# First FFN of a decoder trunk with three pairs of blocks by eight products instead of two, and the low parts of the first gated input's weights made by VectorE and by adding DMAs instead of GpSimd

## The chip, the cores and the metric

The kernel runs on one core of a Trainium2 chip. The metric is the device time of one execution in microseconds (us). The core has a TensorE for matrix products (PE in the profile, its weight loads PEld), VectorE (DVE), ScalarE (ACT), GpSimd (POOL) and SyncE (SP, which here only issues loads). Each takes its own instructions in order and waits for the others at semaphores.

## The reference, cut to what matters

Two layers over 512 tokens of width 1024, everything in float32. Each layer has a half-step gated FFN, a token mixer (retention in the first layer, forgetting attention in the second), another half-step FFN, and a gated input from `p`:

```python
def swiglu(x, w_in, w_out):
    g, u = jnp.split(x @ w_in, 2, axis=-1)
    return (jax.nn.silu(g) * u) @ w_out

h = x
for i in range(DEPTH):                     # DEPTH = 2
    nw = norm_w[i]
    h = h + 0.5 * swiglu(rmsnorm(h, nw[0]), ffn_w_in[i, 0], ffn_w_out[i, 0])
    hn = rmsnorm(h, nw[1])
    h = h + (retention(hn, ...) if i % 2 == 0 else forgetting_attention(hn, ...))
    h = h + 0.5 * swiglu(rmsnorm(h, nw[2]), ffn_w_in[i, 1], ffn_w_out[i, 1])
    gate = jax.nn.sigmoid(rmsnorm(h, nw[3]) @ ple_w_gate[i])
    h = h + gate * (p[i] @ ple_w_proj[i])
return rmsnorm(h, final_norm_w)
```

So there are four FFNs (1024 to 2 x 2816 and back), called 0 to 3 here and "first" to "fourth", and two gated inputs. FFN 0 is the first work of the kernel. The first gated input stands between FFN 1 and FFN 2.

## The kernel before, in words

**Products in three.** The activations lie transposed in SBUF, `h` as eight blocks of 128 features by 512 tokens. Every float32 operand is split into a high part (rounded to the PE's faster float32r) and a low part (the operand less its high part), and a product is made of three matmuls: high by high, high by low, low by high. So each block of weights (128 by 1024, 512 KB, loaded by SP into one of four `wraw` buffers, L76) needs a cast for its high part, on ScalarE (L83), and a low part, in one of two ways. `split` subtracts (L84) on the engine in `W.low`, which is VectorE or, in the mixers and the gated inputs, GpSimd. `negated` writes the negated weights by a second ScalarE pass (L125 is the cast there, L126 the negation) and adds the weights to them by a DMA that reads them a second time and adds on arrival, issued by GpSimd (L127). High and low part go into one of three `w8` buffers (`w` in the profile's rows); the weights are asked for in the order of `W.plan`, a look-ahead of two chunks ahead of their use (`W.look`). A chunk in `W.placed` goes into other buffers than `w8`.

**The FFN's first product.** The 22 column blocks of gate and up are made in 22 "pairs" (gate and up of one block). A pair is a 2 by 2 block product (two halves of the features by two halves of the tokens), and it is made in one of two forms.
- `plain` (L543) makes it by eight block products, 96 matmuls of 256 columns. It needs the normed activations in their plain forms alone, and the weights as two chunks, each with high and low part.
- `start`, `one`, `two`, `three` and `finish` (matmuls in `product`, L508) make it by seven block products, 84 matmuls, in Winograd's way: it needs sums and differences of weight blocks (four sums on VectorE, L157, each split by ScalarE and VectorE into the buffers `s12` and `s34`; a fifth block in `a12` by an adding DMA), and sums and differences of activation blocks (the forms t1 to t4 by `Norm.quarters`, L387 to L420). The results are put together in PSUM by VectorE and ScalarE (L561 to L580).

The first pairs of each FFN are plain, `PLAIN[i]` of them, since the forms take VectorE a while to make; the others are of the seven-product form. The weights of two pairs after the plain ones (and of two at each later seam) are `direct`: their low part is made by subtraction. For each pair `gated` then makes silu(gate) times up (L585 to L590) and splits it; it needs the rows of the norm (`n.rows`), one per token. Those come from sums of squares over the features: `columns` sums them on PE (L337) and takes the root (L479 to L487), and `rows` turns the columns into rows on PE (L474, copied at L468). A plain pair holds two of PSUM's eight banks from its first matmul until it is gated, and a pair of the seven-product form likewise.

**The order at the start of FFN 0.** The input blocks and the first pair's weights arrive in pieces while pair 0 is made. Pair 1's two chunks go into `w8`: the first at once, the second into the buffer that pair 0 gives back. Between pair 0 and pair 1 PE makes the columns. After ten of the sixteen steps of pair 1 it turns them into rows and gates pair 0. Then come pair 2's `one` and `two`, the gating of pair 1, and then, pair by pair, `one` and `two` of the next before `three` of the last.

**The first gated input.** `ple` with `parts == 1` makes eight column blocks of `gate` (24 matmuls each, `ple_g`) and of the added part (6 each, `ple_p`). For each block m, `step` multiplies with the rows (L1131), takes the sigmoid (L1132), multiplies (L1140), adds to `h[m]` (L1141), and makes the forms of block m - 1 for the norm of FFN 2 (`nxt.block`, `corner`: L316, L317, L387 to L420, L440 to L447). Meanwhile `W.low` is GpSimd. From block 4 on the look-ahead is two longer, and the first pair of FFN 2 is placed in buffers that its sums don't use yet (`place_first`: `s34` three times and `a12` once). FFN 2 then runs like FFN 0, with its plain pairs ordered so that the last two feature blocks come last.

**Who orders what.** PE's order is the program's. The order of the other engines' instructions and of the loads is made at build time by a planner from the program's order and its own estimates.

Of the kernel before, what the change touches and what calls it, by code (L numbers as in the profile page):

```python
# [26 lines left out]
FH = 16  # L27
LOOKAHEAD = 2
KEPT = 7
PLAIN = (2, 2, 2, 2)  # L30
CHUNKS = [((0, 6), (6, 14), (14, 22)) for n in PLAIN]
H2 = S // 2
HALVES = (slice(0, H2), slice(H2, S))
# [2 lines left out]
class Pair:  # L36
# [3 lines left out]
    def __init__(self, ffn, q, r):  # L40
        self.ffn, self.q, self.r, self.direct = ffn, q, r, False
# [13 lines left out]
class Weights:  # L55
# [3 lines left out]
    def __init__(self, tc, raw_pool, pool):  # L59
        self.tc, self.nc, self.raw_pool, self.pool = tc, tc.nc, raw_pool, pool  # L60
        self.plan, self.ready, self.used = [], [], 0
        self.low = self.nc.vector
        self.limit, self.spare = None, []
        self.look, self.placed = LOOKAHEAD, {}
        self.sum_pool, self.open_ffn, self.pairs_used = None, None, 0
        self.ahead, self.behind = 0, ()

# [9 lines left out]
        return raw  # L77

    def split(self, raw, hi, lo, src=None):
        if self.low is None and src is not None:  # L80
            self.negated(raw, hi, lo, src)
            return
        self.nc.scalar.copy(hi, raw)  # L83
        self.low.tensor_tensor(out=lo, in0=raw, in1=hi.bitcast(F32), op=ALU.subtract)  # L84

    def chunk(self, src):
        n = src.shape[1]
        raw = self.load(src)
        if id(src) in self.placed:
            hi, lo = (t.rearrange("p a c -> p (a c)") for t in self.placed.pop(id(src))())  # L90
            self.split(raw, hi, lo)
            return hi, lo
        if self.spare:
            tiles = [self.spare.pop(0)() for _ in range(4)]
            for i in range(2):
                self.split(raw[:, 512 * i : 512 * (i + 1)], tiles[i], tiles[2 + i])
            return Halves(tiles[0:2]), Halves(tiles[2:4])
        t = self.pool.tile([P, 2, 1024], F32R, name="w8")
        self.split(raw[:, :n], t[:, 0, :n], t[:, 1, :n], src)
        return t[:, 0, :], t[:, 1, :]  # L100
# [71 lines left out]
    def open(self, ffn, pool):  # L172
        self.open_ffn, self.sum_pool, self.pairs_used, self.ahead, self.behind = ffn, pool, 0, 0, ()

    def place_first(self, pair):

        tile = lambda n, b: self.sum_pool.tile([P, 2, 512], F32R, name=n, bufs=b)
        self.placed[id(pair.q)] = lambda: (tile("s34", 3), tile("s34", 3))
        self.placed[id(pair.r)] = lambda: (tile("s34", 3), tile("a12", 2))
# [19 lines left out]
def trunk(ctx, tc, a):  # L199
    nc = tc.nc  # L200
# [15 lines left out]
    W = Weights(tc, wraw, wpool)  # L216

    def unit(pool):
        return pool.tile([P, S], F32R, name="unit_" + {id(ua): "a", id(ub): "b", id(uc): "c", id(ud): "d"}[id(pool)])


    ffn_src = []
    for i in range(4):
        ins = [Pair(i, a["ffn_w_in"][i, m, 0], a["ffn_w_in"][i, m, 1]) for m in range(NF)]
        chunks = CHUNKS[i]
        outs = [[a["ffn_w_out"][i, m][:, k0 * P : k1 * P] for m in range(KB)] for k0, k1 in chunks]
        for m in [PLAIN[i]] + [k1 + 1 for _, k1 in chunks[:-1]]:
            ins[m].direct = ins[m + 1].direct = True
# [11 lines left out]
    def plan_ffn(i):  # L240
        ins, outs = ffn_src[i]
        at = PLAIN[i]
        for pair in ins[:at]:
# [54 lines left out]
    def bank():  # L298
        return psum.tile([P, S], F32, name="bank")
# [44 lines left out]
    class Norm:  # L344
# [17 lines left out]
        def plain(self, b):  # L362

            g = self.gain[:, b : b + 1]
            if b % 2:
                hi, lo = self.unit(), self.unit()
                split(h[b], hi, lo, g)
                both = [(hi[:, c], lo[:, c]) for c in HALVES]
            else:
                both = []  # L370
                for i, c in enumerate(HALVES):
                    u = self.unit() if i == 0 else unit(ud)
                    both.append(tuple(u[:, d] for d in HALVES))
                    split(h[b][:, c], *both[i], g)
            n = 1 + b % 2
            if n == 1:
                self.forms.append({})
            self.forms[b // 2].update({f"b{n}1": both[0], f"b{n}2": both[1]})
# [139 lines left out]
    def ffn(i, n, nxt, stack, apool, meanwhile=None):  # L518


        ins, outs = ffn_src[i]
# [1 line left out]
        c0, c1 = HALVES  # L523
        live, act = {}, {}

        def plain(m, between=None):

            ws = [W.take(ins[m].q), W.take(ins[m].r)]
            g, u = bank(), bank()
            order = [(k, t) for k in range(KB) for t in range(2)]  # L530
            if i == 2:
                order.sort(key=lambda kt: (kt[0] >= KB - 2, kt[1]))
            elif i:
                order.sort(key=lambda kt: kt[1])
            for at, (k, t) in enumerate(order):
                if at == 10 and between:
                    between()
                e = k % 2
                for o, (w, c) in ((g, (ws[e], 0)), (u, (ws[1 - e], 512))):
                    ks = slice(c + k // 2 * P, c + (k // 2 + 1) * P)  # L540
                    xh, xl = n.forms[k // 2][f"b{1 + e}{1 + t}"]
                    for q, (x, y) in enumerate(((w[0], xh), (w[0], xl), (w[1], xh))):
                        nc.tensor.matmul(  # L543
                            o[:, HALVES[t]], x[:, ks], y, start=k == t == q == 0, stop=k == KB - 1 and q == 2,
                            skip_group_check=True,
                        )
            return g, u
# [61 lines left out]
                    nxt.block(m)  # L609

        done = PLAIN[i]
        whole = [plain(m) for m in range(done - 1)]
        n.columns()
        W.begin((n.last,) if n.early else ())

        def scaled():
            n.rows()
            for m, (g, u) in enumerate(whole):
                gated(m, g, u, True)

        last = plain(done - 1, scaled)
        start(done)
        one(done)
        two(done)
# [2 lines left out]
        for c, (k0, k1) in enumerate(chunks):  # L627
# [8 lines left out]
            done = k1  # L636
# [451 lines left out]
    def ple(l, n, nxt, phi, plo, parts=1):  # L1088

        w = S // parts  # L1090
        with ExitStack() as pools:
# [12 lines left out]
            for part in range(parts):  # L1104
# [52 lines left out]

                m = 0
                if part == 0:
                    W.low = nc.gpsimd  # L1160
                    os = [added(m) for m in range(2 + parts)]
                    gs = gates((0,)) if parts == 1 else gates((0, 1, 2, 3))
                    n.columns()
                    m = len(gs)
                    gs += gates((m,))
                    n.rows()
                    if parts == 1:
                        os += [added(3)]
                        rest(0, gs[0], os[0])
                        gs += gates((2,))  # L1170
                        rest(1, gs[1], os[1])
                        gs += gates((3,))
                    for m in range(2 if parts == 1 else 0, 4):
                        rest(m, gs[m], os[m])
                    m = 4
                    if parts > 1:
                        rest(4, gs[4], added(4))
                        m = 5
                if parts == 1:
                    W.look = LOOKAHEAD + 2  # L1180
                    W.place_first(ffn_src[2][0][0])
                while m < KB:
                    g = gates((m,))[0]
                    rest(m, g, added(m))
# [189 lines left out]
```

## Time and profile before

| | us |
|---|---|
| median of three runs | 2192.59 (2189.26 to 2194.67) |
| the profiled execution | 2193.35 |
| its span in the profile | 2191.5 |
| PE busy | 2142.5 (98%) |
| VectorE busy | 1454.5 (66%) |
| ScalarE busy | 1202.4 (55%) |
| GpSimd busy | 472.6 (22%) |

The profile is of one execution; its times count from the start of the span. In its rows a group or an instruction is named by line, engine, operation, and output<-inputs; "[... <-X]" gives the idle time of the engine just before it and what ended that. A row of a table by stage reads: stretch, length, then busy time and count of instructions for PE, PEld, VectorE, ScalarE and GpSimd, then the granted clock of PE as a share of full speed, the DMA engines' share and GB/s. A row of waits reads: who waited, for whom, us in total, times, the longest.

### The profile page before, as it was taken

How to read it: one execution, taken by the hardware profiler on the slowest of the kernel's cores; microseconds unless marked ns; L12 is line 12 of the kernel's file. 1: busy time of each engine (PE TensorE's matmuls, PEld its weight loads, DVE VectorE, ACT ScalarE, POOL GpSimd, SP SyncE). 2: the span in 40 equal slices, each digit the busy share in tenths (PEclk: the TensorE clock that was granted, in tenths of full speed). 3: DMA queues.
4: the chain of work that ended last, by engine and by line, in shares of the span. 5: the costliest groups of instructions: out<-in, count | busy, mean ns of one | idle time of the engine just before them, and what ended most of it. 6: DMA issues, size and time to landing. Idle time of an engine off the chain costs nothing.

```text
span 2191.5 us, 34456 instructions
## 1 busy us (share of the span) xinstructions
PE 2142.5 (98%) x13525; PEld 1927.9 (88%) x13525; DVE 1454.5 (66%) x2629; ACT 1202.4 (55%) x2027; POOL 472.6 (22%) x354
## 2 busy tenths in 40 slices
PE   8999999999999999999998999999999999999997
PEld 7999997888888798989988999898788899999987
DVE  8686766352533677767758687775675696777765
ACT  7465553433333574745556556464787774655544
POOL 0010003444344000101142011012334200100055
PEclk9999999999999999999999999999999999999999
DMA  5465562222222244746523555463622144654631
GB/s 174 124 167 148 140 164 97 82 95 77 94 77 87 77 128 132 177 119 152 144 94 97 129 160 149 137 167 105 152 81 88 67 125 114 161 154 139 155 106 40
DMA packets 85315, 267.08 MB, mean 122 GB/s; under 512 B 9360, under 2 KB 12944, under 8 KB 85152
## 3 DMA queue, kind: packets, MB, share of 16 engines
q1 hardware_dynamic: 63328, 209.78, 28.2%
q0 software_dynamic: 20592, 54.01, 14.6%
q8 instruction: 106, 1.74, 0.3%
q10 hardware_dynamic: 1232, 1.09, 0.1%
q14 instruction: 57, 0.47, 0.1%
HBM read 262.71 MB, written 2.13 MB: 121 GB/s over the span
## 4 chain that ended last, share of the span: by engine, by line
PE 85%; DVE 6%; ACT 4%; DMA 2%; issue 2%; POOL 1%; SPq 0%; ACTq 0%; DVEq 0%; POOLq 0%
PE bank L508 33%; PE bank L325 14%; PE bank L323 14%; PE bank L324 13%; PE bank L543 4%; PE bank L703 2%; PE bank L702 2%; PE bank L704 2%; DMA wraw<-in_ffn_w_in 1%; ACT p L1006 1%; DVE w L84 1%; ACT p L1008 1%; ACT w L83 1%; DVE tlo L314 1%; PE bank L337 0%
## 5 line engine op out<-in xcount | busy, mean ns | idle before, releaser
L83 ACT CAST w<-wraw 128x1024 fp32r<-128x1024 f32 (+1 forms) x240 | 243.4, 1021 | 420.0 <-PE bank L325 254.9
L325 PE MATMUL bank<-unit_a,w 128*128 128x512 f32 x736 | 287.2, 390 | 4.3 <-DVE w L84 2.6
L323 PE MATMUL bank<-unit_a,w 128*128 128x512 f32 x736 | 288.5, 392 | 1.9 <-ACT w L83 1.6
L324 PE MATMUL bank<-unit_a,w 128*128 128x512 f32 x736 | 286.7, 390 | 0.2 <-DVE unit_a L314 0.2
L84 POOL TENSOR_TENSOR w<-wraw,w 128x1024 fp32r<-128x1024 f32 x93 | 226.8, 2442 | 259.3 <-ACT w L83 246.8
L83 ACT CAST s<-sums 128x512 fp32r<-128x512 f32 x320 | 191.8, 617 | 153.4 <-DVE sums L157 107.4
L325 PE MATMUL bank<-unit_d,w 128*128 128x512 f32 (+1 forms) x712 | 268.2, 377 | 4.6 <-DVE w L84 4.6
L323 PE MATMUL bank<-unit_d,w 128*128 128x512 f32 (+1 forms) x712 | 269.3, 378 | 3.2 <-ACT w L83 1.6
L324 PE MATMUL bank<-unit_d,w 128*128 128x512 f32 (+1 forms) x712 | 268.0, 376 | 1.8 <-DVE unit_d L314 1.8
L84 DVE TENSOR_TENSOR s<-sums,s 128x512 fp32r<-128x512 f32 x320 | 214.1, 685 | 75.8 <-ACT s L83 75.3
L127 POOL DMA_DIRECT2D a<-in_ffn_w_in x80 | 70.3, 878 | 643.4 <-ACT a L126 422.0
L84 DVE TENSOR_TENSOR w<-wraw,w 128x1024 fp32r<-128x1024 f32 (+1 forms) x147 | 173.3, 1184 | 19.5 <-ACT w L83 19.3
L508 PE MATMUL bank<-unit_b,s 128*128 128x256 f32 x880 | 184.4, 276 | 0.7 <-DVE bank L565 0.7
L508 PE MATMUL bank<-unit_d,s 128*128 128x256 f32 x1140 | 178.4, 276 | 0.0
L508 PE MATMUL bank<-unit_a,s 128*128 128x256 f32 x1260 | 175.0, 276 | 1.4 <-ACT unit_a L387 0.9
L604 DVE SCALAR_TENSOR_TENSOR tmp<-bank,rows 128x512 f32<-128x512 f32 x96 | 66.0, 689 | 164.9 <-PE bank L325 163.7
L325 PEld LDWEIGHTS bank<-unit_a,w 128*128 128x128 f32 x736 | 138.1, 188 | 35.5 <-DVE w L84 4.3
L323 PEld LDWEIGHTS bank<-unit_a,w 128*128 128x128 f32 x736 | 138.2, 188 | 32.2 <-ACT w L83 3.5
L324 PEld LDWEIGHTS bank<-unit_a,w 128*128 128x128 f32 x736 | 138.2, 188 | 28.5 <-DVE unit_a L314 0.5
L325 PEld LDWEIGHTS bank<-unit_d,w 128*128 128x128 f32 x712 | 134.3, 189 | 30.7 <-DVE w L84 6.6
L323 PEld LDWEIGHTS bank<-unit_d,w 128*128 128x128 f32 x712 | 134.4, 189 | 30.2 <-ACT w L83 3.3
L508 PEld LDWEIGHTS bank<-unit_a,s 128*128 128x128 f32 x1260 | 158.0, 188 | 1.8 <-ACT unit_a L387 1.1
(292 smaller groups left out, 4787.9 us busy)
## 6 DMA issues: line engine op xcount, KB each, us to landing
wraw<-in_ffn_w_in SPq DMA_DIRECT2D x174, 512.0 KB, 4.3
wraw<-in_ffn_w_out SPq DMA_DIRECT2D x64, 512.0 KB, 4.7
w<-in_ffn_w_in POOLq DMA_DIRECT2D x56, 512.0 KB, 5.4
a<-in_ffn_w_in POOLq DMA_DIRECT2D x80, 256.0 KB, 6.3
wraw<-in_ffn_w_out SPq DMA_DIRECT2D x32, 384.0 KB, 3.7
wraw<-in_ret_qk SPq DMA_DIRECT2D x16, 512.0 KB, 3.5
wraw<-in_ret_v SPq DMA_DIRECT2D x16, 512.0 KB, 3.6
wraw<-in_ret_g SPq DMA_DIRECT2D x16, 512.0 KB, 3.5
```

The costliest lines, as they stand in the source:

```text
L83: self.nc.scalar.copy(hi, raw)
L84: self.low.tensor_tensor(out=lo, in0=raw, in1=hi.bitcast(F32), op=ALU.subtract)
L127: self.nc.gpsimd.dma_start(out=lo, in_=src, accum_op=ALU.add)
L323: nc.tensor.matmul(out, wh, xh, start=first, stop=False)
L324: nc.tensor.matmul(out, wh, xl, start=False, stop=False)
L325: nc.tensor.matmul(out, wl, xh, start=False, stop=last)
L508: add = lambda w, x, start, stop: nc.tensor.matmul(out, w, x, start=start, stop=stop, skip_group_check=True)
L543: nc.tensor.matmul(o[:, HALVES[t]], x[:, ks], y, start=k == t == q == 0, stop=k == KB - 1 and q == 2, skip_group_check=True,)
L604: nc.vector.scalar_tensor_tensor(out=t1, in0=o, scalar=-0.5, in1=n.r, op0=ALU.mult, op1=ALU.mult)
L702: nc.tensor.matmul(os[t], xh, wh[:, js], start=k == 0, stop=False)
L703: nc.tensor.matmul(os[t], xh, wl[:, js], start=False, stop=False)
L704: nc.tensor.matmul(os[t], xl, wh[:, js], start=False, stop=k == KB - 1)
```

## The change

- FFN 0 has three plain pairs and not two (`PLAIN[0]`), and its two direct pairs are then pairs 3 and 4.
- In FFN 0 the look-ahead is two longer while pair 0 is made, and pair 1's two chunks are placed in the buffers `s34` and `a12` (`place`, which was `place_first`).
- In FFN 0 the columns are made inside pair 1, ahead of its step 12 of 16, and the rows in pair 2 at step 10, with the gating of pairs 0 and 1. The other FFNs keep their order.
- In the first gated input `W.low` is VectorE and not GpSimd. The second gated input keeps GpSimd.
- The four chunks of the first two pairs of FFN 2 are marked in `W.by_dma`: their low parts are made by `negated`, also where the chunk is placed.

```diff
-PLAIN = (2, 2, 2, 2)
+PLAIN = (3, 2, 2, 2)
...
     def split(self, raw, hi, lo, src=None):
-        if self.low is None and src is not None:
+        if src is not None and (self.low is None or id(src) in self.by_dma):
             self.negated(raw, hi, lo, src)
             return
...
             hi, lo = (t.rearrange("p a c -> p (a c)") for t in self.placed.pop(id(src))())
-            self.split(raw, hi, lo)
+            self.split(raw, hi, lo, src)
...
-        whole = [plain(m) for m in range(done - 1)]
-        n.columns()
-        W.begin((n.last,) if n.early else ())
+        if i:
+            whole = [plain(0)]
+            n.columns()
+            W.begin((n.last,) if n.early else ())
+        else:
+            W.look = LOOKAHEAD + 2
+            W.place(ins[1])
+            whole = [plain(0)]
+            W.look = LOOKAHEAD
+            whole.append(plain(1, {12: n.columns}))
+            W.begin(())
 
         def scaled():
             n.rows()
             for m, (g, u) in enumerate(whole):
                 gated(m, g, u, True)
 
-        last = plain(done - 1, scaled)
+        last = plain(done - 1, {10: scaled})
...
                 if part == 0:
-                    W.low = nc.gpsimd
+                    W.low = nc.gpsimd if parts > 1 else nc.vector
...
                     W.look = LOOKAHEAD + 2
-                    W.place_first(ffn_src[2][0][0])
+                    W.place(ffn_src[2][0][0])
+                    W.by_dma |= {id(x) for pair in ffn_src[2][0][:2] for x in (pair.q, pair.r)}
```

More of the change, by code (lines that the diff above doesn't have):

```diff
@@ L63, in __init__ @@
         self.limit, self.spare = None, []
-        self.look, self.placed = LOOKAHEAD, {}
+        self.look, self.placed, self.by_dma = LOOKAHEAD, {}, set()
         self.sum_pool, self.open_ffn, self.pairs_used = None, None, 0
@@ L173, in open, with place @@
         self.open_ffn, self.sum_pool, self.pairs_used, self.ahead, self.behind = ffn, pool, 0, 0, ()
-    def place_first(self, pair):
+    def place(self, pair):
         tile = lambda n, b: self.sum_pool.tile([P, 2, 512], F32R, name=n, bufs=b)
@@ L524, in ffn, with plain @@
         live, act = {}, {}
-        def plain(m, between=None):
+        def plain(m, between={}):
             ws = [W.take(ins[m].q), W.take(ins[m].r)]
@@ L535, in plain @@
             for at, (k, t) in enumerate(order):
-                if at == 10 and between:
-                    between()
+                if at in between:
+                    between[at]()
                 e = k % 2
```

## The prediction

> **What bounds the kernel now.** I read the page's head first, then busy time by stage, then what TensorE waited for in each stage with holes, then the timelines of the other engines there.
>
> ```profile
> span 2191.5 us, 34456 instructions
> PE 2142.5 (98%) x13525; PEld 1927.9 (88%) x13525; DVE 1454.5 (66%) x2629; ACT 1202.4 (55%) x2027; POOL 472.6 (22%) x354
> ```
>
> TensorE (PE) is busy 98% of the span: nearly everywhere time is its stream of products, and a change can pay only where that stream has holes or runs at a low clock. The two edits touch two such places: the start of the first FFN, and the passage from the first gated input (its last product ends at 1169.2) into the third FFN. By stage (length, PE busy, weight load, VectorE, ScalarE, GpSimd, then the granted clock):
>
> ```profile
> 26.20:39.60 13.40, 13.40 (x101) 13.40 (x102) 13.40 (x36) 12.41 (x25) 1.93 (x2) 0.88 0.37 78
> 39.60:54.10 14.50, 10.74 (x87) 9.94 (x85) 13.98 (x27) 11.10 (x18) 0.88 (x1) 1.00 0.58 167
> 70.00:87.50 17.50, 17.50 (x155) 17.50 (x154) 14.81 (x27) 11.76 (x22) 1.98 (x3) 1.00 0.72 173
> ...
> 1169.20:1188.40 19.20, 13.62 (x106) 12.52 (x104) 18.85 (x32) 12.61 (x24) 4.76 (x2) 1.00 0.24 68
> 1188.40:1201.90 13.50, 13.50 (x103) 13.50 (x103) 10.22 (x21) 7.82 (x13) 0.89 (x1) 0.87 0.46 137
> ```
>
> In the holes VectorE is the full engine: 13.40 of 13.40, 13.98 of 14.50, 18.85 of 19.20. What PE waited for, first in 22 to 55 us, then in 1100 to 1200 us:
>
> ```profile
> PE bank L337 <- ACT tmp L313: 2.2, 1, 2.2
> PE bank L508 <- ACT tmp L564: 1.7, 1, 1.7
> PE bank L508 <- ACT unit_a L387: 0.9, 1, 0.9
> PE bank L508 <- DVE bank L565: 0.7, 1, 0.7
> PE bank L337 <- DVE tmp L314: 0.5, 1, 0.5
> PE bank L508 <- DVE unit_a L388: 0.4, 1, 0.4
> ...
> PE bank L543 <- DVE unit_a L317: 2.9, 2, 1.4
> PE bank L543 <- ACT unit_c L387: 1.3, 1, 1.3
> PE bank L337 <- DVE tmp L314: 1.1, 1, 1.1
> PE bank L543 <- DVE unit_c L388: 0.3, 1, 0.3
> ```
>
> That is 6.4 us at the start and 5.6 us at the passage.
>
> **The change part by part. Units.** Twelve products of the eight-product form take 1.43 us at full clock (start 1198.29, next group 1199.72), 0.119 us each:
>
> ```profile
> 1198.29 1.60 PE L543 MATMUL bank<-unit_d,w 128*128 128x256 f32 x12
> 1199.72 0.28 PE L543 MATMUL bank<-unit_c,w 128*128 128x256 f32 x1
> ```
>
> In the seven-product form the window 70 to 87.5 gives 17.5/155 = 0.113 us. A pair by eight products is 96 matmuls, 11.4 us; by seven it is 84, 9.5 us. Turning the third pair costs 1.9 us of PE.
>
> **First FFN, what is lost now.** From the end of the first pair (22.3) to the point from which PE never stops again (54.1) are 31.8 us. The work in it: 96 products (11.4), the token sums and the turning of the columns (twelve short products, about 0.1 each as an estimate from the unit: 1.2), and 84 products of the seven form (9.5): 22.1. So 9.7 us are lost: the 6.4 of waits, 13.40 x (1 - 0.88) = 1.6 by the clock after the hole, and 1.7 of restarts.
>
> ```profile
> 21.99 1.99 ACT L83 CAST w<-wraw 128x1024 fp32r<-128x1024 f32 x2 [3.82 <-PE bank L543]
> 23.07 1.23 DVE L84 TENSOR_TENSOR w<-wraw,w 128x1024 fp32r<-128x1024 f32 x1 [1.20 <-ACT w L83]
> 36.45 0.58 ACT L468 COPY rows<-bank 128x512 f32<-128x512 f32 x1
> 47.28 0.68 DVE L585 TENSOR_TENSOR tmp<-bank,rows 128x512 f32<-128x512 f32 x1
> 50.01 0.68 DVE L588 SCALAR_TENSOR_TENSOR tmp<-bank,tmp 128x512 f32<-128x512 f32 x1
> ```
>
> Pair 1's second half is cast only at 21.99: ScalarE stood 3.82 us for a weight buffer that PE gave back at the first pair's end, and everything behind that cast in its queue, the forms for the seven products too, stood with it. With pair 1 in the sums' buffers that wait goes: cast at about 18.2, low part at about 20 to 23. PE can start pair 1 at 22.3; I charge 0.4 for the low part (ends 0 and 0.8: 23.07, now the time of pair 1's second low part, less 22.3). The columns move into pair 1 at step 12, 72 x 0.119 = 8.6 us in; they need the squares' low part, done before 26.2 now, so the 2.2 and 0.5 go. Behind that wait on PE stand only pair 1's last 24 products.
>
> Pair 2 by eight products needs two casts and two low parts (2 x 1.23 of VectorE); by seven it needed four sums and four low parts of 0.68 (the size of L1131 below) and one of 1.23: VectorE is relieved by 6.7 - 2.5 = 4.2 us. PE reaches pair 3 at about 22.7 + 11.4 + 1.2 + 11.4 = 46.7 instead of pair 2 at 39.6, with the forms (the waits of 0.9 and 0.4 now) done. Late next: banks. Three open pairs and pair 3 fill all eight, so pair 4, due at 46.7 + 36 x 0.113 = 50.8, needs pair 0 closed. Today the rows are there at 37.0 and pair 0 is closed at 50.7, because VectorE does forms and sums first. The rows would now come at about 43; at today's lag pair 0 closes at 56.7, 5.9 late; with a free VectorE it takes 50.7 - 47.3 = 3.4 and is in time. Waits in these steps are 3.7 us now; I keep 1.4.
>
> Sum: -9.7 + 1.9 + 0.4 + 1.4 = **-6.0** us. Ends: -7.8 (nothing kept) and -9.7 + 1.9 + 0.8 + 5.9 = -1.1. On the queues: SP issues the same loads, each raw buffer freed as early or earlier; GpSimd loses pair 2's adding DMA and, as the direct pairs are now 3 and 4, pair 4's. One pair more is gated before the rest, none in all.
>
> **First gated input, what is lost now.** From 1169.2 to 1201.9, 32.7 us, PE has 192 products (22.8) and 1.2 of small ones: 8.7 us are lost, 5.6 in waits, 13.5 x (1 - 0.87) = 1.8 by the clock, 1.3 in restarts. VectorE is late there, and its rows say why (1130 to 1190):
>
> ```profile
> L1141 DVE TENSOR_TENSOR hall<-hall,tmp 128x512 f32<-128x512 f32 x8 | 10.6, 1320 | 0.0
> L414 DVE SCALAR_TENSOR_TENSOR tmp<-tmp 128x256 f32<-128x256 f32 x4 | 5.8, 1441 | 1.8 <-ACT tmp L407 1.8
> L1131 DVE TENSOR_TENSOR tmp<-bank,rows 128x512 f32<-128x512 f32 x8 | 5.4, 680 | 4.0 <-ACT rows L468 4.0
> ```
>
> In 1200 to 2000, at the next norm of this kind, L414 reads:
>
> ```profile
> L414 DVE SCALAR_TENSOR_TENSOR tmp<-tmp 128x256 f32<-128x256 f32 x4 | 1.7, 416 | 0.0
> ```
>
> L1141 is as large as L1131 and takes twice as long; L414 takes 1441 ns and not 416. The long ones lie under GpSimd's subtractions:
>
> ```profile
> 1151.56 2.67 POOL L84 TENSOR_TENSOR w<-wraw,w 128x1024 fp32r<-128x1024 f32 x1 [1.75 <-ACT w L83]
> 1151.89 2.88 DVE L1141 TENSOR_TENSOR hall<-hall,tmp 128x512 f32<-128x512 f32 x1
> ...
> L84 POOL TENSOR_TENSOR w<-wraw,w 128x1024 fp32r<-128x1024 f32 x10 | 25.2, 2530 | 27.1 <-ACT w L83 23.1 <-issue 4.0
> ```
>
> Twelve go (these ten, and the two of pair 0). The stretch that goes in the first two rows is 10.6 - 8 x 0.68 + 5.8 - 4 x 0.42 = 9.3 us. Eight low parts of this projection come to VectorE, 1.23 each; four fall before 1138, where VectorE waits anyway (the 4.0 in L1131's row), so 4.9 us are added: 4.4 net of the 5.6 that PE waits, and more where shorter operations were stretched too.
>
> The third FFN's first two pairs go by a second ScalarE pass (1.03 each, 4.1 us on an engine busy 12.61 of 19.2) and an adding DMA:
>
> ```profile
> 1173.83 1.03 ACT L83 CAST w<-wraw 128x1024 fp32r<-128x1024 f32 x1
> L84 POOL TENSOR_TENSOR a<-wraw,s x1: 2894/2894/2894, 1154.2 to 1154.2; 128x1024 fp32r<-128x1024 f32 x1
> L127 POOL DMA_DIRECT2D w<-in_ffn_w_in x56: 872/875/893, 44.1 to 2049.2; - x56
> w<-in_ffn_w_in POOLq DMA_DIRECT2D x56, 512.0 KB, 5.4
> ...
> 1190.81 0.89 POOL L127 DMA_DIRECT2D a<-in_ffn_w_in  x1 [12.89 <-ACT a L126]
> ```
>
> Pair 0's second half has its GpSimd work at 1154.2 now; by DMA it lands at about 1154.2 + 1.0 + 0.9 + 5.4 = 1161.5, 7.7 us ahead of need. Pair 1's second half is tight: cast at 1173.83 now, landing at 1173.83 + 2 x 1.03 + 0.9 + 5.4 = 1182.2, and PE would want it at 1169.2 + 11.4 + 0.8 = 1181.4. I keep 2.2 us in all: 0.8 for this, 0.6 for the last forms, 0.8 for the clock and restarts. Sum: -8.7 + 2.2 = **-6.5** us. Ends: -8.7, and -1.5 (that half 5 us later, with the clock lost again).
>
> [...]
>
> The profiled execution took 2193.35 us, 1.85 outside its span; the median of the runs is 2192.59, 0.8 lower. 2193.35 - 6.0 - 6.5 = 2180.9: **2181 us**. The gain is 0.6%; about 0.3% (6.6 us) is what a measurement can tell from no change.
>
> **The rivals.**
> - Pair 1's adding DMA becomes the new wait. GpSimd issues in order, and a DMA of this kind can stand behind another's wait. A landing at 1186 leaves the passage with about -2; with the start that is -8, 2185. [...] Against: its buffer comes free with the projection's last gate, before 1169.2, and today's cast at 1173.83 is late for VectorE's reasons.
> - Banks. Pair 4 waits for pair 0's close, the start gives -1.1, the passage -6.5: 2186. For it: today's lag of 10 us behind the rows. Against: 4 us less for VectorE there.
> - The change doesn't do what it says: VectorE takes the low parts in order, each waiting for its cast, and the forms stay as late; the third pair's 1.9 is paid for half of the start's waits. About -2, 2191. Against: the stretch of 9.3 us is twice the 4.9 that comes.
> - Slower: GpSimd's queue holds pair 3's adding DMA ahead of pair 1's. That one goes out at 1190.8 now (last row above); behind it pair 1 lands at 1190.8 + 0.9 + 0.9 + 5.4 = 1198, 10 us after today's start of that pair at 1188.4. Passage +10, less the start's 6.0: 2197. It makes the kernel slower from a landing of 1194.4 on (1188.4 + 6.0), by over 0.3% from 1201. Against: pair 3 is asked for after pair 1.
>
> **How the numbers follow.** Forecast, both parts near their sums: 0.52 (2177 to 2185). Late DMA 0.16, banks 0.12, nothing gained 0.12, slower 0.06, other 0.02. Faster by over 0.3% holds for the forecast nearly whole (0.50), for half of the late DMA and more than half of the banks (0.17), and for a little beside: 0.70. Slower 0.05: half of the last rival, landing later still, and 0.02 for holes that no row here shows. The rest, 0.25, is no change. The range runs from both best ends (2193.35 - 16.5 = 2177) to the case of nothing gained (2190), which leaves out a fifth.
>
> **What would show it.** Right: no wait of PE at L337 for L313 near 22 us; pair 1's products following pair 0's within 1 us, granted clock near 1.0 from 20 to 45 us; no stop of pair 4 for a bank; L1141 at 0.68 us and no GpSimd subtraction between 1110 and 1180; pair 1 of the third FFN about 11.5 us behind pair 0. Wrong: a wait at L543 for an adding DMA, or at L508 for L588; long idle of VectorE for ScalarE's casts inside the projection; new holes elsewhere, since the order on the other engines is planned anew for the whole kernel, which no row of before can show.

## The result, and the profile after

The changed kernel takes 2182.54 us (median; 2178.86 to 2183.75), the kernel before 2192.59 us: ratio 0.9956, 95% interval 0.9941 to 0.9970, that is 6.6 to 12.9 us less. The page of its profiled execution (2182.19 us):

```profile
span 2180.4 us, 34464 instructions
PE 2138.2 (98%) x13537; PEld 1925.9 (88%) x13537; DVE 1446.2 (66%) x2627; ACT 1201.6 (55%) x2022; POOL 443.0 (20%) x344
```

PE does twelve matmuls more (the third plain pair has 96 for 84) in 4.3 us less busy time. Its clock was halved in five stretches of 3.41 us before and in two after, the one at the kernel's end not counted. GpSimd is busy 29.6 us less.

**The start of FFN 0.** Windows of the changed kernel (length, PE, weight load, VectorE, ScalarE, GpSimd, granted clock, DMA share and GB/s):

```profile
19.90:31.50 11.60, 11.39 (x100) 11.20 (x99) 11.07 (x19) 8.67 (x15) 1.05 (x1) 1.00 0.68 204
32.30:44.20 11.90, 11.90 (x102) 11.90 (x101) 11.90 (x31) 10.89 (x21) 0.88 (x1) 1.00 0.39 111
44.20:52.60 8.40, 8.40 (x75) 8.40 (x75) 8.40 (x15) 8.01 (x14) 0.87 (x1) 1.00 0.50 140
52.60:60.00 7.40, 5.71 (x49) 5.51 (x48) 7.30 (x13) 5.88 (x9) 0.87 (x1) 1.00 0.76 140
```

The windows are pair 1 with the columns in it, pair 2, the first products of pairs 3 and 4, and what follows. Up to the last window PE stops once, for 0.2 us. The hole is in the last window, and the waits of PE up to 80 us name it:

```profile
PE bank L508 <- DVE bank L565: 1.7, 1, 1.7
PE bank L308 <- DVE tmp L306: 1.6, 1, 1.6
PE bank L543 <- DVE w L119: 0.7, 2, 0.5
PE bank L543 <- DVE a L84: 0.2, 1, 0.2
```

The 0.2 is pair 1's low part, the 1.7 VectorE's addition at L565, for which PE waits until 55.85. The waits at L308 and for L119 lie ahead of pair 1 and stood in the kernel before too (1.6 and 1.1 us). Of the gain, 3.4 us are the clock. Two stretches of the kernel before:

```profile
15.71:19.12 3.41, 3.41 (x18) 3.41 (x18) 3.41 (x7) 2.46 (x4) 0.00 (x0) 0.50 0.84 278
25.95:29.36 3.41, 3.41 (x18) 3.41 (x18) 3.41 (x10) 3.38 (x7) 1.05 (x1) 0.50 0.58 155
```

and in the changed kernel:

```profile
15.71:19.12 3.41, 3.41 (x31) 3.41 (x30) 3.41 (x6) 3.15 (x4) 0.00 (x0) 1.00 0.64 237
25.95:29.36 3.41, 3.41 (x33) 3.41 (x31) 2.94 (x8) 3.41 (x8) 1.05 (x1) 1.00 0.51 183
```

Twice 3.41 us at a clock of 0.50 is 3.4 us lost before; after, none is lost there. The first output block of FFN 0, before and then after:

```profile
87.47 0.40 PE L323 MATMUL bank<-unit_d,w 128*128 128x512 f32 x1
```
```profile
79.55 0.40 PE L323 MATMUL bank<-unit_d,w 128*128 128x512 f32 x1
```

7.9 us earlier: 3.4 by the clock, 4.5 by waits and restarts net of the 1.9 of the third pair.

**The passage to FFN 2.** Of 5.6 us of waits one is left, in the columns. VectorE's rows have their short times (L1149 of the changed kernel is L1141 of the kernel before), and the last adding DMA of pair 1 goes out at 1168.34. Shown are the waits of 1100 to 1200, VectorE's rows of 1110 to 1195, GpSimd's timeline, and the first plain pair as a window:

```profile
PE bank L337 <- DVE tmp L314: 1.1, 1, 1.1
```
```profile
L84 DVE TENSOR_TENSOR w<-wraw,w 128x1024 fp32r<-128x1024 f32 x10 | 12.2, 1222 | 6.2 <-ACT w L83 6.2
L1149 DVE TENSOR_TENSOR hall<-hall,tmp 128x512 f32<-128x512 f32 x8 | 5.5, 684 | 0.0
...
L414 DVE SCALAR_TENSOR_TENSOR tmp<-tmp 128x256 f32<-128x256 f32 x4 | 1.7, 421 | 1.0 <-ACT tmp L407 1.0
```
```profile
1168.34 0.88 POOL L127 DMA_DIRECT2D w<-in_ffn_w_in  x1 [4.84 <-ACT w L126]
```
```profile
1165.60:1177.40 11.80, 11.70 (x97) 11.31 (x95) 11.43 (x22) 10.49 (x19) 1.75 (x2) 1.00 0.80 157
```

This DMA lands at 1175.8, and pair 1 starts at 1179.56. From FFN 2's first plain product to its first seven-product group are 25.98 us, 32.70 before: 6.7 us less.

**Where the 11.1 us of the span came from.** Starts of products on PE, after less before, in the profiled executions:

| place | before | after | shift |
|---|---|---|---|
| FFN 0, first output block | 87.47 | 79.55 | -7.9 |
| FFN 0, third chunk's first pair | 244.37 | 236.46 | -7.9 |
| FFN 0, third output block | 317.65 | 315.36 | **-2.3** |
| FFN 1, first product | 771.03 | 767.19 | -3.8 |
| FFN 2, first product | 1169.18 | 1165.59 | -3.6 |
| FFN 2, first seven-product group | 1201.88 | 1191.57 | -10.3 |
| FFN 3, first product | 1772.58 | 1760.97 | -11.6 |
| end | 2191.55 | 2180.42 | -11.1 |

Both edits gave what the traces of their places say, and 5.6 us of the first were given back 200 us later, inside FFN 0's third chunk (its last group of pairs). PE there, and ScalarE:

```profile
289.33 0.50 PE L508 MATMUL bank<-unit_a,s 128*128 128x256 f32 x3
292.87 0.86 PE L508 MATMUL bank<-unit_a,w 128*128 128x256 f32 x5 [3.04 <-ACT tmp L564]
```
```profile
289.52 0.62 ACT L83 CAST s<-sums 128x512 fp32r<-128x512 f32 x1 [3.17 <-DVE sums L157]
290.05 1.04 ACT L125 CAST w<-wraw 128x1024 fp32r<-128x1024 f32 x1
291.00 1.05 ACT L126 ACTIVATE w<-wraw 128x1024 fp32r<-128x1024 f32 x1
291.95 0.60 ACT L83 CAST s<-sums 128x512 fp32r<-128x512 f32 x1
292.46 0.36 ACT L564 COPY tmp<-bank 128x256 f32<-128x256 f32 x1
```

PE waits for the copy at L564. ScalarE had that copy fourth in line behind a cast that waited 3.17 us for VectorE's sums; and the sums waited 3.02 us for a raw load issued at 281.71, landed at 288.60: 6.9 us, beside two adding DMAs. A stretch of 3.41 us at half clock follows at 294.27. Whether this loss belongs to the change is what the last group of experiments asks.

### The profile page after: what moved, and what is told of

Same layout as the page of the kernel before. It is cut to its first block, busy times and chain, and to the rows that moved or that the text cites. A ratio compares the mean times of both kernels' runs of the same rounds, so it can differ in the third digit from the quotient of the medians.

```text
span 2180.4 us, 34464 instructions
## 1 busy us (share of the span) xinstructions
PE 2138.2 (98%) x13537; PEld 1925.9 (88%) x13537; DVE 1446.2 (66%) x2627; ACT 1201.6 (55%) x2022; POOL 443.0 (20%) x344
## 4 chain that ended last, share of the span: by engine, by line
PE 83%; DVE 6%; ACT 5%; DMA 3%; issue 2%; POOL 0%; SPq 0%; DVEq 0%; ACTq 0%; POOLq 0%
PE bank L508 31%; PE bank L325 14%; PE bank L323 14%; PE bank L324 14%; PE bank L543 3%; DMA wraw<-in_ffn_w_in 3%; PE bank L710 2%; PE bank L711 2%; PE bank L712 2%; DVE w L84 1%; ACT p L1014 1%; DVE tlo L314 1%; ACT w L83 1%; ACT p L1016 1%; DVE sums L157 1%
## 5 line engine op out<-in xcount | busy, mean ns | idle before, releaser
L84 DVE TENSOR_TENSOR s<-sums,s 128x512 fp32r<-128x512 f32 x316 | 211.8, 686 | 75.0 <-ACT s L83 74.8
L84 POOL TENSOR_TENSOR w<-wraw,w 128x1024 fp32r<-128x1024 f32 x83 | 201.4, 2429 | 232.5 <-ACT w L83 224.0
L127 POOL DMA_DIRECT2D a<-in_ffn_w_in x80 | 70.1, 876 | 645.5 <-ACT a L126 452.4
L84 DVE TENSOR_TENSOR w<-wraw,w 128x1024 fp32r<-128x1024 f32 (+1 forms) x155 | 183.1, 1186 | 22.5 <-ACT w L83 22.3
L508 PE MATMUL bank<-unit_a,s 128*128 128x256 f32 x1224 | 170.4, 276 | 0.0
L325 PEld LDWEIGHTS bank<-unit_d,w 128*128 128x128 f32 x712 | 134.2, 188 | 30.5 <-DVE w L84 6.6
L323 PEld LDWEIGHTS bank<-unit_d,w 128*128 128x128 f32 x712 | 134.2, 188 | 30.1 <-ACT w L83 3.2
L324 PEld LDWEIGHTS bank<-unit_d,w 128*128 128x128 f32 x712 | 134.2, 188 | 26.3 <-DVE unit_d L314 3.2
```

The costliest lines, as they stand in the source:

```text
L127: self.nc.gpsimd.dma_start(out=lo, in_=src, accum_op=ALU.add)
L323: nc.tensor.matmul(out, wh, xh, start=first, stop=False)
L324: nc.tensor.matmul(out, wh, xl, start=False, stop=False)
L325: nc.tensor.matmul(out, wl, xh, start=False, stop=last)
L508: add = lambda w, x, start, stop: nc.tensor.matmul(out, w, x, start=start, stop=stop, skip_group_check=True)
```

## Experiments

The theory: the two edits pay separately, each in its own place, the start by pair 1's room, the moved columns and the third pair together, the passage by VectorE freed of GpSimd's subtractions; what the start loses again is lost to loads that land late beside adding DMAs. Rivals stand in the expectations. Each run is compared with the kernel before on the same chip (medians 2190.68, 2192.38 and 2192.70 us in the three groups of runs).

**Each edit alone.** The first run takes the gated input's lines back:

```diff
-                    W.low = nc.gpsimd if parts > 1 else nc.vector
+                    W.low = nc.gpsimd
-                    W.by_dma |= {id(x) for pair in ffn_src[2][0][:2] for x in (pair.q, pair.r)}
```

> The FFN 0 part alone; the gated input keeps its subtractions on GpSimd and FFN 2's first chunks lose their adding DMAs. Theory: FFN 0's start wins some 8 us and its third chunk gives 5.6 us of it back in every execution, because the raw weights of pairs 17 to 21 land late where their loads overlap adding DMAs; so retention starts 2.3 us earlier, TensorE waits again for L564's copy in 270 to 300 us (some 3.4 us), and the time is 2190.3 us, ratio 0.999. Rival one: the wait in the third chunk was an accident of one execution; then this profile has no wait for L564 and the time is 2192.6 - 7.9 = 2184.7. Rival two: the 2.4 us of pair 0 (its products at half speed before, at full speed after) belong to the execution and not to the kernel; then the profile shows FFN 0's first output block at 82 instead of 79.6 us.

Measured: 2186.62 us, ratio 0.9982 [0.9973, 0.9992], or -3.9 us. In the profile the first block stands at 79.27 and all 8.2 us are still there at the start of FFN 1 (762.84): no wait in the third chunk. So "in every execution" is wrong, and the second rival too. But the median is not the 2184.7 of the first rival either: the profiled execution, with 2183.43, was the quickest of the twelve, and the run lies between theory and rival.

The second run has the gated input's lines and PLAIN, columns and begin as before.

> The gated input's part alone, FFN 0 as before. Theory: the passage from the gated input to FFN 2 gives its 6.7 us by itself, and with the 1 to 2 us that the stretches around it gave the time is 2184 to 2186 us, ratio 0.9965. Rival: the passage is worth that only with the other part in (the order on the other engines is planned anew); then 2188 us or more. On pair 0 of FFN 0: if its half-speed products belong to the old order of the start, this profile ends pair 0 at 22.3 us as before; if they are the chip's accident, it ends at 20 us.

Measured: 2184.69 us, 0.9972 [0.9961, 0.9983], -6.1 us: the theory. The passage took 27.00 us, 5.7 less than before, with one half-clock stretch in it. Pair 0 of FFN 0 ran at full clock here and ended near 20 us, so where the half speed stands belongs to the execution; but two half-clock stretches came all the same (3.4 us), one behind the other from 22.11 on, in the columns and pair 1, and the first block stands at 86.42. The edits add up as far as the intervals tell: 3.9 + 6.1 = 10.0 us (each with some 2 us to either side), and together they gave 10.05 in the medians, 11.8 in the second comparison below.

**Inside the gated input's edit.** The run with VectorE's low parts alone drops the by_dma line; the run with adding DMAs alone keeps that line and has W.low = nc.gpsimd. Both are without the FFN 0 part.

> Of the gated input's part only the move of the low parts to VectorE; the four chunks of FFN 2's first two pairs are subtracted by VectorE too, so no adding DMA stands in the passage. Theory (the stretched VectorE operations were the loss): TensorE's waits for VectorE in 1169 to 1202 us go, and the four chunks add four subtractions of 128x1024 to VectorE, at most some 3 us of which part shows; 2186 to 2189 us, L1141 at 0.68 us. Rival (the adding DMA is the part that pays): VectorE is now the late engine, TensorE waits for VectorE's w L88 or L84 by 4 us or more, and the time is 2190 us or more.

> Of the gated input's part only the adding DMAs for FFN 2's first two pairs; the other chunks of the first gated input keep their subtractions on GpSimd. Theory: GpSimd's subtractions up to some 1150 us still stretch VectorE (L1141 at 1 us or more in the mean), but the four that stood latest, beside the norm of FFN 2, are gone: about half of the passage's gain, 2188 to 2190 us. Rival (the adding DMA is all of it): 2185 to 2186 us and no TensorE wait over 1 us in the passage. Second rival: the adding DMAs, issued by GpSimd behind its subtractions, come late, and TensorE waits at L543 for one; 2193 us or more.

Measured: 2189.47 us, 0.9992 [0.9982, 1.0003], and 2189.96 us, 0.9991 [0.9981, 1.0001]: neither is told from no change by its time. The first lies 0.5 above its theory, without the waits of the rival; the second is at the upper end of its theory, with L1141 shorter than was expected there. In the passage itself each does its part. VectorE's rows and PE's waits (1100 to 1200) with VectorE's low parts alone:

```profile
L1141 DVE TENSOR_TENSOR hall<-hall,tmp 128x512 f32<-128x512 f32 x8 | 5.5, 684 | 0.0
```
```profile
PE bank L337 <- DVE tmp L314: 1.0, 1, 1.0
PE bank L543 <- ACT unit_c L387: 0.8, 1, 0.8
PE bank L543 <- DVE unit_c L388: 0.4, 1, 0.4
```

and with the adding DMAs alone:

```profile
L1141 DVE TENSOR_TENSOR hall<-hall,tmp 128x512 f32<-128x512 f32 x8 | 6.7, 837 | 0.0
...
L414 DVE SCALAR_TENSOR_TENSOR tmp<-tmp 128x256 f32<-128x256 f32 x4 | 3.8, 949 | 6.2 <-ACT tmp L407 6.2
```
```profile
PE bank L337 <- DVE tmp L314: 1.1, 1, 1.1
PE bank L543 <- DVE unit_a L317: 1.0, 1, 1.0
PE bank L543 <- ACT unit_c L387: 0.4, 1, 0.4
PE bank L543 <- DVE unit_c L388: 0.3, 1, 0.3
```

The stretch goes with GpSimd's subtractions (L1141: 1320 ns before, 837 with eight of them left, 684 with none), and the waits go from 5.6 to 2.2 and to 2.8 us; with both, 1.1. At full clock the old passage took 31.07 us (the FFN 0 part alone), VectorE's low parts alone 27.00, both 25.98; the adding DMAs alone 29.65 with one half-clock stretch in it, so about 27.9 without (an estimate, 1.7 less). Of the 5.1 us that both give, the low parts by VectorE alone give 4.1 and the adding DMAs alone some 3.1: the two overlap, as both take away subtractions of GpSimd, the first all twelve, the second four. Of its 4.1 the run with the low parts alone shows only 1.2 us in its median. Its profiled execution took 2.4 us longer than that of the whole edit from FFN 2's first seven-product group to FFN 3, and 2.9 us longer behind that, in places that the edit doesn't touch; it has three half-clock stretches more (5.1 us). Why its median holds so little stays open.

**Inside the start's edit.** Three plain pairs and nothing else:

```diff
-PLAIN = (2, 2, 2, 2)
+PLAIN = (3, 2, 2, 2)
```

> The kernel before with PLAIN 3 for FFN 0 and nothing else: the columns and the sums still stand between plain pairs, here after the second, and pair 1's weights wait for the w8 buffers. Theory: the third plain pair is only the means; what pays is that nothing stands between pair 0 and pair 1 and that pair 1's weights have room. So the stop of TensorE moves behind pair 1 or falls between pair 0 and pair 1 as a wait for w L83/L84 or a DMA, the gain at FFN 0's first output block is 0 to 4 us instead of 8, and the time is 2189 to 2193 us beside 2191 before. Rival: more plain work alone covers the norm; then the block starts 7 us or more earlier and the time is as that of the FFN 0 part, 2186.6 us, ratio 0.998.

Measured: 2192.66 us, 0.9998 [0.9987, 1.0010]: the theory. The first block is 1.6 us earlier, and PE's waits say what took the rest:

```profile
PE bank L543 <- DVE w L84: 2.8, 2, 1.9
PE bank L543 <- ACT w L83: 1.9, 2, 1.5
```

More plain work alone doesn't cover the norm: its own weights come late. With pair 1 placed, columns still between the pairs:

```diff
+        if i == 0:
+            W.look = LOOKAHEAD + 2
+            W.place_first(ins[1])
         whole = [plain(m) for m in range(done - 1)]
+        if i == 0:
+            W.look = LOOKAHEAD
```

> The kernel before with three plain pairs and pair 1's weights placed; the columns stay whole between the second and the third plain pair, and the sums begin there. Against the run with three pairs alone this adds the placing, against the FFN 0 part alone it lacks only the columns' place inside pair 1. Theory (three pairs without placing stopped for w L83/L84 of the third pair's weights, 3.4 us of waits and a clock of 0.66): with the placing these waits go, the first output block stands at 79.5 to 80.5 us and the time is as the FFN 0 part's, ratio 0.998. Rival (the columns' place inside pair 1 is needed): TensorE stops between the pairs for the columns or the sums come 1.5 us later and pair 3 waits for them; the block at 82 to 85 us, ratio 0.999 to 1.0.

Measured: 2189.44 us, 0.9985 [0.9975, 0.9995]: the rival. These waits are gone, the block stands at 82.81, 4.7 us earlier than before, and there are two others:

```profile
PE bank L474 <- DVE cols L483: 2.3, 1, 2.3
PE bank L508 <- ACT tmp L564: 1.0, 1, 1.0
```

PE comes to turn the columns into rows ten steps after it has summed them, and stands there for VectorE, which is late with the root. With the columns inside pair 1 that chain lies under products. Third, both moves with two plain pairs (columns after six steps of pair 1, rows after twelve):

> The FFN 0 part alone, but with two plain pairs: pair 1's weights placed in the idle sums' buffers, the norm's columns inside pair 1 after six of its steps, its rows after twelve; the gated input as before. Theory (the third pair is needed as cover): the columns have no stop, but the sums of pair 2, begun only behind them, are late; TensorE waits 4 us or more for L83/L84 of s ahead of pair 2's second product or for unit_a of the norm; the first output block comes at 82 us or later, the time is 2189 to 2192 us beside 2192 before. Rival (placing and the moved columns are all that is needed): no wait of 1 us or more in 20 to 50 us, the block at 77 to 78 us, since a plain pair costs 1.9 us more, and the time is 2184 to 2186 us.

Measured: 2192.14 us, 0.9995 [0.9983, 1.0006]; the first block at 85.35: the theory's time and place, though the waits stand elsewhere than it said:

```profile
PE bank L474 <- DVE cols L483: 2.6, 1, 2.6
PE bank L508 <- ACT tmp L564: 2.6, 1, 2.6
```

So the steps pay in full only together. At the first block three pairs give 1.6 us, placing 3.0 more, the columns' place 3.5 more (82.81 to 79.27); without the third pair both moves give 2.1. These counts hold the clock too: two half-clock stretches stand ahead of the block with three pairs alone, one with placing, none with all, at up to 1.7 us each. And the old start's block stood at 86.38 to 87.47 in four profiles, so the smallest of them is uncertain by 1 us.

**What is given back.** The changed kernel once more:

> The changed kernel once more, unedited, beside the others on the same chip. Theory (the 5.6 us lost in FFN 0's third chunk are an accident of one execution, of which the same program showed 0 us in another): the first output block of FFN 0 at 79.5 us again, the third chunk's loss anywhere from 0 to 6 us, the median 2182 to 2184 us, ratio 0.996. Rival (the loss belongs to the program): 5 to 6 us lost there again, waits for L564 of 3 us.

Measured: 2180.61 us, 0.9949 [0.9934, 0.9963]. First block at 79.55; third chunk's loss 2.0 us. Three executions with the same program up to there lost 5.6, 2.0 and 0 us. PE in 280 to 300 us: the changed kernel, again, and the FFN 0 part alone:

```profile
280.00:300.00 20.00, 16.96 (x131) 16.76 (x132) 14.79 (x29) 12.20 (x23) 2.86 (x4) 0.91 0.72 158
```
```profile
280.00:300.00 20.00, 18.26 (x159) 18.06 (x158) 15.03 (x28) 12.63 (x24) 2.62 (x3) 1.00 0.74 183
```
```profile
280.00:300.00 20.00, 20.00 (x176) 20.00 (x175) 16.38 (x31) 13.44 (x24) 2.91 (x4) 1.00 0.78 200
```

The loss is not in the program's order but in what an execution does with it. In the changed kernel's profile the load issued at 257.19 already lands in 7.1 us, where its like takes 4.1 in the execution without loss (issued at 256.90); in the second one, which lost 2.0, it takes 4.2 as well, so that load is not the whole story. It isn't new either: the seven profiles with the old start or parts of the new one lost 0 to 1.6 us there.

Then the adding DMAs are taken out of that chunk, x's low part first (six of 256 KB), and in another run the first products' (five of 512 KB):

```diff
-            self.negated(a12, pair.x[:, 0, :], pair.x[:, 1, :], pair.r[:, 0:512])
+            low = self.split if pair.late else self.negated
...
+        if i == 0:
+            for m in range(16, NF):
+                ins[m].late = True
```
```diff
+        if i == 0:
+            for m in range(17, NF):
+                ins[m].direct = True
```

> The changed kernel, with the low part of a12 (x) of pairs 16 to 21 of FFN 0 subtracted by VectorE: six adding DMAs of 256 KB, and ScalarE's six passes L126 for them, are gone from the third chunk. Theory (the third chunk loses some 2 to 6 us in many executions to loads that land late beside adding DMAs): the load after the sums is issued earlier and lands in 4 to 5.5 us instead of 7, no wait for L564 of 1 us or more, and the median is 2 to 4 us under that of the changed kernel run beside it. Rival one (the accidents are spread over the whole run, and the third chunk is but one place): no difference, within 1 us of it. Rival two (VectorE, 15 of 20 us busy there, becomes the late engine): TensorE waits for DVE L565 or L84 by 1 us and more per pair and the median is 2 us or more above it.

> The changed kernel, with pairs 17 to 21 of FFN 0 direct: their first products' low part by VectorE (one subtraction of 128x1024 for each, some 1.2 us) in place of ScalarE's second pass and an adding DMA of 512 KB. Theory: as for x's low part, and more so, since an adding DMA of 512 KB takes 5 to 6 us of every 9.7: no wait for L564, median 2 to 4 us under the changed kernel's. Rival one: no difference. Rival two: VectorE has some 2.4 us of 9.7 free for each pair, half of them go, and it becomes late: TensorE waits at L508 for DVE, 2 us or more slower.

Measured: 2176.88 us, 0.9933 [0.9919, 0.9948], and 2179.99 us, 0.9947 [0.9934, 0.9960]. Beside the changed kernel's 2180.61 the first is the theory in its time (-3.7), the second the rival of no difference (-0.6). Neither profile has a wait for that copy in the chunk, and the chunk keeps the whole gain of the start; the second has one of 1.5 us in FFN 1's third chunk. To part the adding DMAs from ScalarE's second passes, which went with them, a run keeps the passes and lets VectorE add:

```diff
+            if pair.late:
+                nc.scalar.copy(hi, a12)
+                nc.scalar.mul(lo, a12, -1.0)
+                nc.vector.tensor_tensor(out=lo, in0=lo.bitcast(F32), in1=a12, op=ALU.add)
```

> As the run with x's low part by VectorE in FFN 0's third chunk, but ScalarE keeps both of its passes for x (copy, and times -1); VectorE adds in the place of the adding DMA. It parts the two things that the move took away: six adding DMAs of 256 KB, and six passes of ScalarE. Theory (the adding DMAs, which slow the loads): loads of the third chunk land in 4.1 us in the mean (5.5 to 5.8 with the DMAs), no wait for L564 of 1 us, the time as with x's low part by VectorE, 2177 us. Rival (ScalarE's queue is the chain): loads land as early, but the passes keep the raw buffers, and the waits for L564 of 1 to 3 us stay; 2180 to 2181 us as the changed kernel.

Measured: 2179.61 us, 0.9946 [0.9933, 0.9958]. Median microseconds to landing of the chunk's loads (244 to 308): the changed kernel again, x's low part by VectorE, and with ScalarE's passes kept:

```profile
wraw<-in_ffn_w_in SPq DMA_DIRECT2D x7, 512.0 KB, 6.5
```
```profile
wraw<-in_ffn_w_in SPq DMA_DIRECT2D x7, 512.0 KB, 4.3
```
```profile
wraw<-in_ffn_w_in SPq DMA_DIRECT2D x7, 512.0 KB, 3.5
```

The landing follows the adding DMAs, not ScalarE's passes, and with early loads no wait stands in the chunk, passes or not: as far as the profile goes, the theory. Over all profiles those loads take 5.2 to 6.9 us in the median with all the adding DMAs (ten) and 3.5 to 4.6 without six or five of them (four). But of the ten, three have no loss in the chunk (the kernel before, the FFN 0 part alone, and three pairs with pair 1 placed), so late loads make the wait possible, not certain, and four profiles without one are few. The time lies between the two expectations and doesn't decide. Last, x's low part by VectorE in the third chunks of all four FFNs:

> The changed kernel with x's low part by VectorE in the third chunk of all four FFNs instead of FFN 0's alone. Theory (late loads beside adding DMAs cost each third chunk something; waits for L564 of 0.3 to 2.2 us stood in FFN 1 to 3 in the runs so far): 1 to 4 us under the run with FFN 0's alone, 2173 to 2176 us, and no wait for L564 of 1 us anywhere. Rival: the three other chunks have slack, within 1 us of FFN 0's alone, 2177 us. Second rival: VectorE, with the norm's or the head's work beside it at the end of an FFN, becomes late there: 2179 us or more.

Measured: 2177.56 us, 0.9932 [0.9919, 0.9945]: the first rival; the time shows nothing to win in FFN 1 to 3. Yet single executions do wait there for that copy: in FFN 1's third chunk (1000 to 1100 us) by 0.4 us in the changed kernel, 0.9 in its second profile, 1.5 and 2.4 in the runs with the products' low part and with ScalarE's passes kept, 2.0 and 1.1 with three pairs alone and with pair 1 placed; behind 1195 us most profiles do, by up to 2.2 us in all. This run's profile has no such wait anywhere.

The version with x's low part by VectorE in FFN 0's third chunk is 3.7 us under the changed kernel beside it in the median (2174.72 to 2181.85 against 2178.81 to 2184.47); the ratios' intervals to the kernel before still overlap, so that it is quicker than the kernel before is shown, and that it is quicker than the changed kernel is likely.

## Why the prediction was right, and where it was not

2181 us were forecast, 2182.54 and 2180.61 measured; the range held both. From the medians of the kernel before these are gains of 10.1 and 11.8 us, where the sum had 12.5 from the profiled execution. By its steps:

- **Pair 1's room.** Forecast: pair 1 about 0.4 us behind pair 0. Measured: one wait of 0.2 at its low part; and without this room three pairs are worth nothing in the median. Right.
- **Columns at step 12.** The waits of 2.2 and 0.5 went, as said. The runs add what the prediction had not priced: with three pairs and pair 1 placed, 3.5 us hang on that place, 2.3 of it a wait of PE for the columns' root and 1.7 a half-clock stretch behind it (other waits differ by the rest).
- **The third pair, 1.9 us of PE.** Paid; with two pairs only 2.1 of the 7.9 us came.
- **Kept waits, 1.4.** 1.7 at L565. No stop for a bank: pair 4 followed pair 3 at 48.41, and that rival fell.
- **The clock, 1.6.** This term was mis-sized. The prediction saw one low-clock stretch (26 to 29 us); another lay inside pair 0 (15.71 to 19.12), which it took for pair 0's normal length. Every profile with the old start, with three pairs alone or with two pairs and both moves (six) has two such stretches up to the first block, not always in the same place; the seven with the whole new start have none. Hence -7.9 for -6.0 at the first block.
- **What is gained at the start arrives at the end.** This was assumed without a word, but for the warning of new holes, and is the step that failed. The first block came 7.9 us earlier, the median only 3.9 us (1.8 to 5.9). Shown are two places of give-back: FFN 0's third chunk, 0 to 5.6 us by execution, and FFN 1's third chunk, with waits of 0 to 2.4 us where the kernel before has none. They don't account for all of it: what else the typical execution loses stays open.
- **The passage, -6.5.** -6.7 in the profile, -6.1 by the run of its own. L1141 at 684 ns, L414 at 421, the subtractions now on VectorE at 1.22 us: as forecast. Its make-up was other than written: 5.1 us at equal clock (31.07 to 25.98) and 1.6 for a half-clock stretch that only some executions have; four of the seven profiles with the whole edit of the gated input have one there too. The sign "about 11.5 us behind pair 0" did not come: pair 1 follows by 13.97, since the columns and their wait of 1.1 stand between the pairs.
- **The late adding DMA.** Forecast landing 1182.2 for a need at 1181.4; it landed at 1175.8 for a need at 1179.6. ScalarE's cast for it came at 1166.04 and not at 1173.83, probably since the VectorE work that it stood behind was no longer late. That rival and the slower one (GpSimd's order) fell: the next adding DMA behind pair 1's last went out at 1172.87. The landing itself took 7.5 us where 5.4 were put in. The two issues at L127 in 1165.60 to 1177.40 took 0.88 us each beside a VectorE busy 11.43 of 11.80 us, within the 872 to 893 ns of the kernel before, so nothing stretched them here.

The two errors were of opposite sign: the start gave more than its sum (7.9 for 6.0), and less of it arrived (3.9). That the total came so close is in part luck.

## What to carry to other kernels

In this kernel the hole at the FFN's start was closed only when the weights' room, the place of the norm's chain and the work that covers it were changed together; one or two of them moved the stop to the next wait. When PE gets ahead, look at the next long loop that was just in time: here loads of 512 KB landed in 5.2 to 6.9 us (median) beside all the adding DMAs and in 3.5 to 4.6 with six or five of them gone, which kept the gain in that loop in all four profiles. Of the three runs with that change in FFN 0 alone, only one was more than 1 us quicker than the changed kernel (3.7 us). And size a hole with the half-clock stretch that it can set off, here 1.7 us for each 3.41 us of it, since removing the wait removes the chance too: two stretches up to FFN 0's first block with the old start, none with the whole new one.

## What the runs showed of the hardware

The clock loss comes in pieces of one size, on a fixed grid. In all fourteen profiles each low stretch, but for the last one at the kernel's end, lasts 3.41 us or two or three times that, at 0.50: 1.7 us lost for each 3.41. The same wait sets one off in one execution and not in the next: in retention, behind a wait of 1.7 us for GpSimd's w L84, the changed kernel ran at full clock, and the run with x's low part in all FFNs ran eight products at half speed:

```profile
374.01:377.42 3.41, 3.41 (x17) 2.82 (x16) 2.72 (x2) 0.62 (x2) 1.64 (x1) 1.00 0.59 177
```
```profile
368.30:371.71 3.41, 3.41 (x10) 2.67 (x9) 2.70 (x2) 0.64 (x2) 1.62 (x1) 0.53 0.54 181
```

From FFN 0's third output block to FFN 1 the fourteen profiles took 451.8, 453.4 or 455.0 us and nothing between, with none, one or two such stretches. That is a good part of the spread of 5 to 12.5 us between executions of one kernel, and of what a single profile can be off by: ahead of the last one at the end, the quickest profiled execution (2174.72) has no such stretch, the slowest (2198.19) eight.

In every profile the stretches begin whole multiples of 3.413 us apart, to 0.004: in the kernel before at 15.71, 25.95, 739.33, 1189.89 and 2121.73, which are 3, 209, 132 and 273 multiples. Laid over PE's products in the fourteen traces, this grid has 19 cells in which the products left 1.84 us or more uncovered, and a low stretch follows every one; with less, some are followed and others not. This suggests, though no run tested it, that a wait counts by how much of it falls into one cell, and that short ones add up: the stretch at 739.33 follows a cell with waits of 0.30, 0.52 and 0.59 us. Retention's wait of 1.7 us stands in all fourteen profiles: in eight it is split over two cells, and no stretch follows; in six it lies in one cell, and a stretch follows in four of them. Why not in the other two stays open.

VectorE was slowed beside GpSimd's subtractions by a factor of 1.9 at L1141 (128x512, 1320 against 684 ns) and of 3.4 at L414 (128x256, 1441 against 421 ns); where GpSimd only issues adding DMAs the short times stand. L1131 in the same stretch, with one of its two inputs in a PSUM bank, took 680 ns before and 683 after.

That PE is faster in float32r than in float32, as the kernel's description has it, was not shown: no run makes these products in float32.
